# Channel shuffle on one core: twelve tiles of 38 KB in place of fifteen of 32, with two store buffers instead of three

## The chip, the cores and the metric

The kernel runs on one core of a Trainium2 chip; the other cores are idle. The metric is device time in microseconds (us), as the median of a few executions. The profile is of one execution; its span, from the first to the last instruction, is some 1.8 us shorter than the time.

"KB a partition" is how much of a tile lies in each of the 128 partitions: a tile of 32 KB is 128 rows of 32 KB, so 4096 KB in all.

## The reference

```python
x = x.reshape(batch, h, w, groups, channels_per_group)   # 16, 64, 64, 8, 32
x = x.transpose(0, 1, 2, 4, 3)
x = x.reshape(batch, h, w, c)                            # float32, c = 256
```

Nothing is computed. Each pixel's 256 channels are read as 8 groups of 32 and written as 32 groups of 8. 67.11 MB must come in and 67.11 MB must go out.

## The kernel before

A tile is loaded, VectorE copies it into another buffer in the new order, and it is stored. Loads are issued from SyncE, stores from ScalarE, so each has a queue of its own on the 16 DMA engines. The tile framework adds the waits: load n+3 waits for copy n (three load buffers), copy n waits for load n and for store n-3 (three store buffers).

```python
_SIZES = [4, 8, 16] + [32] * 15 + [4]     # KB a partition; sums to 512
_IN_BUFS = 3
_OUT_BUFS = 3
# ... (pools, views)
for q in _SIZES:
    in_tile = in_pool.tile([P, biggest * c], F32, name="in_tile")
    nc.sync.dma_start(out=in_tile[:, : q * c], in_=rows(x_flat, first, q))
    out_tile = out_pool.tile([P, biggest * c], F32, name="out_tile")
    nc.vector.tensor_copy(
        out=out_tile[:, : q * c].rearrange("p (i j g) -> p i j g", j=CPG, g=G),
        in_=in_tile[:, : q * c].rearrange("p (i g j) -> p i j g", g=G, j=CPG),
    )
    nc.scalar.dma_start(out=rows(out_flat, first, q), in_=out_tile[:, : q * c])
    first += P * q
```

## Time and profile before

| | before |
|---|---|
| time, median of 3 | 316.96 us |
| span of the profile | 315.2 us |
| VectorE busy | 119.9 us, 38% |
| packets of both queues, share of 16 engines' time | 49.8% + 49.4% |
| mean rate | 426 GB/s |
| DMAs | 19 loads, 19 stores |

The page's lines for these stand in the prediction. How to read them: look for the unit that is never free. VectorE isn't it; the DMA engines are, in all slices but the first and the last.

### The profile page before, as it was taken

To read this page: it belongs to the slowest core of one execution; us is meant where nothing else is said; L and a number is where in the kernel's file an instruction comes from. 1 tells how busy PE (TensorE), PEld (TensorE's weight loads), DVE (VectorE), ACT (ScalarE), POOL (GpSimd) and SP (SyncE) were. 2 spreads that over 40 slices of the span, in tenths; PEclk is the share of its full clock that TensorE was granted. 3 is DMA by queue.
4 is the path that set the end of the run, shared out by engine and by line. 5 is a ranking of instruction groups with operands and counts; after the bars stand their busy time and mean duration, and the time that the engine had idled before them with its cause. 6 is when DMAs were issued, how large, how long until landed. Compare 5 with 4: busy or idle time off the path is not lost.

```text
span 315.2 us, 150 instructions
## 1 busy us (share of the span) xinstructions
DVE 119.9 (38%) x19; POOL 0.2 (0%) x4
## 2 busy tenths in 40 slices
DVE  2419270905318062270722608135090440905500
POOL 0000000000000000000000000000000000000000
DMA  8999999999999999999999999999999999999996
GB/s 314 408 422 458 403 449 408 457 408 453 412 453 412 458 412 453 420 445 428 437 428 437 437 428 437 428 437 433 437 433 437 428 441 424 445 420 426 439 441 291
DMA packets 5472, 134.22 MB, mean 426 GB/s; under 512 B 608, under 2 KB 608, under 8 KB 1120
## 3 DMA queue, kind: packets, MB, share of 16 engines
q1 hardware_dynamic: 2736, 67.11, 49.8%
q10 hardware_dynamic: 2736, 67.11, 49.4%
HBM read 67.11 MB, written 67.11 MB: 426 GB/s over the span
## 4 chain that ended last, share of the span: by engine, by line
DMA 40%; another core or an unknown queue 30%; DVE 25%; issue 0%; DVEq 0%; SPq 0%
DMA in_tile<-in_x_dram 40%; DVE out_tile L49 25%; DVEq L49 0%; SPq L47 0%
## 5 line engine op out<-in xcount | busy, mean ns | idle before, releaser
L49 DVE COPY out_tile<-in_tile 128x8192 f32<-128x8192 f32 (+3 forms) x19 | 119.9, 6313 | 179.3 <-DMA in_tile<-in_x_dram 179.3
L71 POOL MEMSET const-uint8-127<- 128x1 uint8 x1 | 0.1, 103 | 0.0
L71 POOL MEMSET const-bfloat16-1.0<- 128x1 bf16 x1 | 0.1, 102 | 0.0
L71 POOL MEMSET const-float32-0.0<- 128x1 f32 x1 | 0.1, 99 | 0.2 <-issue 0.2
L71 POOL MEMSET const-float32-1.0<- 128x1 f32 x1 | 0.1, 99 | 0.0
## 6 DMA issues: line engine op xcount, KB each, us to landing
in_tile<-in_x_dram SPq DMA_DIRECT2D x15, 4096.0 KB, 50.5
out_dram<-out_tile ACTq DMA_DIRECT2D x15, 4096.0 KB, 42.4
in_tile<-in_x_dram SPq DMA_DIRECT2D x1, 2048.0 KB, 11.1
out_dram<-out_tile ACTq DMA_DIRECT2D x1, 2048.0 KB, 30.1
in_tile<-in_x_dram SPq DMA_DIRECT2D x2, 512.0 KB, 22.7
in_tile<-in_x_dram SPq DMA_DIRECT2D x1, 1024.0 KB, 5.5
out_dram<-out_tile ACTq DMA_DIRECT2D x2, 512.0 KB, 14.4
out_dram<-out_tile ACTq DMA_DIRECT2D x1, 1024.0 KB, 22.9
```

What stands on the lines that cost most here:

```text
L49: nc.vector.tensor_copy(out=out_tile[:, : q * c].rearrange("p (i j g) -> p i j g", j=CPG, g=G), in_=in_tile[:, : q * c].rearrange("p (i g ...
L71: nc = _bacc.Bacc("TRN2", target_bir_lowering=False, num_devices=1)
```

## The change

The intent: larger transfers, so fewer of them and less overhead, in the same memory. Three load and two store buffers of 38 KB take 190 KB a partition, where three and three of 32 KB took 192. The three small tiles ahead stay, the small one at the end goes.

```diff
-_SIZES = [4, 8, 16] + [32] * 15 + [4]
+_SIZES = [4, 8, 16] + [38] * 12 + [28]
 _IN_BUFS = 3
-_OUT_BUFS = 3
+_OUT_BUFS = 2
```

## The prediction

> **What bounds the kernel now.** I read the page first (busy shares, then the slices, then the queues), then the DMA view, the waits, the copies by shape, the timeline and at last windows over the end.
>
> From the page of the kernel before: busy time of the engines, the DMA share in 40 slices, and the two queues (q1 loads, q10 stores) with packets, MB and share of the 16 DMA engines' time.
>
> ```profile
> DVE 119.9 (38%) x19; POOL 0.2 (0%) x4
> ...
> DMA  8999999999999999999999999999999999999996
> ...
> q1 hardware_dynamic: 2736, 67.11, 49.8%
> q10 hardware_dynamic: 2736, 67.11, 49.4%
> ```
>
> VectorE, the only engine that computes, works 38% of the span. The DMA engines are at 90% or more in 38 of 40 slices, and the two queues' packets add up to 49.8 + 49.4 = 99.2% of all the time that 16 engines have in 315.2 us. So the kernel is bound by its transfers, and only the first and the last slice have room in them.
>
> The waits (us in total, times, longest) and the copies by shape (count, busy us, mean ns, idle before):
>
> ```profile
> DVE out_tile L49 <- DMA in_tile<-in_x_dram: 179.3, 19, 11.9
> ```
>
> ```profile
> L49 DVE COPY out_tile<-in_tile 128x8192 f32<-128x8192 f32 x15 | 111.9, 7459 | 166.2 <-DMA in_tile<-in_x_dram 166.2
> L49 DVE COPY out_tile<-in_tile 128x4096 f32<-128x4096 f32 x1 | 3.8, 3835 | 4.1 <-DMA in_tile<-in_x_dram 4.1
> ```
>
> All 19 waits of VectorE are put down to loads. None is put down to a store, so three store buffers are enough today. But a wait names only what came last; the DMA view (count, KB each, median us from issue to landing) shows how near the stores are:
>
> ```profile
> in_tile<-in_x_dram SPq DMA_DIRECT2D x15, 4096.0 KB, 50.5
> out_dram<-out_tile ACTq DMA_DIRECT2D x15, 4096.0 KB, 42.4
> ...
> out_dram<-out_tile ACTq DMA_DIRECT2D x2, 512.0 KB, 14.4
> ```
>
> A store is 42.4 us in flight, and in the timeline the copies start 19.4 us apart (267.84, 287.23). So a store buffer is held for 7.5 + 42.4 = 49.9 of the 58.1 us that three buffers allow. With two it could not be held so long: that is the risk of this change.
>
> The timeline of the last copies and two windows at the end (busy of VectorE, of GpSimd, clock, DMA share, GB/s):
>
> ```profile
> 267.84 7.45 DVE L49 COPY out_tile<-in_tile 128x8192 f32<-128x8192 f32 x1 [11.91 <-DMA in_tile<-in_x_dram]
> 287.23 7.47 DVE L49 COPY out_tile<-in_tile 128x8192 f32<-128x8192 f32 x1 [11.95 <-DMA in_tile<-in_x_dram]
> 298.20 1.09 DVE L49 COPY out_tile<-in_tile 128x1024 f32<-128x1024 f32 x1 [3.50 <-DMA in_tile<-in_x_dram]
> ```
>
> ```profile
> 300.00:305.00 5.00, 0.00 (x0) 0.00 (x0) 1.00 1.02 439
> 310.00:315.00 5.00, 0.00 (x0) 0.00 (x0) 1.00 0.55 229
> ```
>
> The last copy ends at 299.3 and the last packet of a store at 313.9 (packet records of the trace). For those 14.6 us the stores run alone, and they still move 439 GB/s: one queue fills the engines as well as two. So neither of the queues must be full; what costs time is only a stretch in which **both** are empty.
>
> **What the Trainium skill says.** Four places.
> 1. "DMA: Bandwidth & Descriptors", Where 436 GB/s comes from: it gives a ceiling of 435.2 GB/s for the 16 engines. The trace agrees: one tile in and one out, 2 x 4.194 MB every 19.36 us, is 433 GB/s. There is next to nothing above it.
> 2. The same page, Rules for kernel authors: for top bandwidth, 128 partitions and at least 1 MiB a DMA. The bulk transfers here are 4 MiB already, so the rule promises nothing for larger ones; the packet times below agree.
> 3. The same page, Queues, rings and completion order: an engine takes turns between its queues packet by packet. In the packet records one row of one partition is one packet, and the turns show: a 512 KB store takes 14.4 us (median) when its 4 KB rows alternate with much longer load rows. Eight rows an engine at 1.21 + 0.16 us a pair are 11.0 us, the rest is the way to the first packet and receipt.
> 4. "SBUF — State Buffer", Specifications (TRN2): 224 KiB a partition, about 208 usable. Before takes (3 + 3) x 32 = 192 KB, after (3 + 2) x 38 = 190 KB, so it fits. No run has yet shown it.
>
> **The change, part by part.**
>
> *Rows of 38 KB, fewer packets.* The packet records give fixed durations when the engines are full: 4 KB 159 ns, 8 KB 309, 16 KB 611, 32 KB 1213, and 9 ns for the completion packet of each engine and DMA. (1213 - 159) / 28 = 37.64 ns a KB, which leaves 159 - 4 x 37.64 = 8 ns fixed. A 38 KB row is then 8 + 38 x 37.64 = 1439 ns, a 28 KB row 1062 ns (estimates from that line). Each engine moves 8 rows of every DMA. Per queue and engine:
> before: 15 x 8 x 1.213 + 8 x (0.159 + 0.309 + 0.611 + 0.159) + 19 x 0.009 = 145.56 + 9.90 + 0.17 = 155.63 us;
> after: 12 x 8 x 1.439 + 8 x (0.159 + 0.309 + 0.611 + 1.062) + 16 x 0.009 = 138.14 + 17.13 + 0.14 = 155.41 us.
> Two queues: 311.27 against 310.82, so **0.45 us less**. All of this lies on the path, since the engines are full; but it is all that six DMAs fewer are worth.
>
> *Larger copies.* (7459 - 3835) / 4096 elements = 0.885 ns an element with 0.21 us fixed. A 38 KB tile (9728 elements) takes 8.82 us, a 28 KB tile (7168) 6.55 us. VectorE's sum falls from 119.9 by three fixed costs, about 0.6 us, to 119.3. The beat becomes 16 x 1.439 + 0.02 = 23.04 us, so the copy still fits in it. All beside the transfers: nothing.
>
> *Two store buffers.* Copy n now waits until store n-2 has landed. At the start the loads of 4, 8 and 16 KB land as before (by 12.4 us), but store 0, with 4 KB rows alternating with 38 KB load rows, lands at some 20 us, so the copy of the 16 KB tile starts near 20.5 instead of 12.74. Store 1 takes 8 x (1.439 + 0.309) = 14.0 us more, store 2 16.4 us, and from there on stores take 23.0 each. So the copies fall into step with the *stores*: store n-2 lands, copy n runs 8.8 us, store n queues behind store n-1. A store is then 2 x 23.04 - 8.8 - 0.5 = 37 us in flight. Meanwhile loads run ahead: at copy n two further loads are out or landed, and load n+3 is issued when the copy ends. While copy n runs, store n-1 has its packets in the queue. Both queues are never empty together, and what one leaves the other takes. Cost: 0 in the middle.
>
> *The end.* The last tile is 28 KB instead of 4. Loads finish first, then stores have the engines alone, and a 38 KB store takes 8 x 1.439 = 11.5 us. The chain that must fit beneath it: receipt of store n-2 to start of copy 0.5 us (as between last completion packet of a load and copy), copy 8.82, issue to first packet 1.1 us (the first load was issued at 0.73, its first packet is at 1.75). For tile 14 that is 10.4, for the last 6.55 + 1.6 = 8.2 us. Both are under 11.5, so the engines stay full: cost 0, with 1.1 us to spare at the tighter place.
>
> *Sum.* First packet at 1.75 as before; 310.82 us of packets; the 0.85 us of gaps that before has (first packet to last 312.12, less 311.27), which I take over; 1.28 us from the last packet to the end of the span: 314.7 against 315.2. The median has 1.8 us more than the span, so **316.5 us**.
>
> **Rivals.** (a) *The two store buffers starve the engines.* For it: 49.9 us of holding against 46.1 us that two buffers allow, so VectorE will certainly wait for stores. Against it: a wait of VectorE costs nothing while packets are queued, and by the reckoning above some always are. If the tighter place in the tail is missed by 2 us and the start loses 1 to 2, it comes to 318 to 320 us, still within 2%. (b) *The 28 KB tail is exposed*: if store 14 were done before the last copy is, up to the whole 8.2 us would show, 325 us, which is over 2% slower. It needs loads that finish last; the loads lead by nearly three tiles, so I hold it unlikely. (c) *Larger rows are faster, or slower, than the line says.* Faster by over 2% would need some 440 GB/s, more than any steady window has; 32 KB rows have only 8 of 1213 ns that could be saved. Slower (a long row cut into pieces, a row pitch that the memory likes less) nothing in the trace suggests.
>
> **Range and chances.** The sum gives 316.5; the runs of before spread by 0.3. Upward I leave room for a microsecond of gaps at start or end: 316.0 to 317.5. A gain of over 2% would need 310.6, below the packets' own time with the start and end: 1%. Over 2% slower needs rival (b) or a slow row: 2%.
>
> **What would show it.** Packets 16 x 144 = 2304 a queue; the share of the two queues again near 99%; copies at 8.8 us and 23.0 us apart. VectorE's waits should now be mostly on stores, while the DMA slices stay at 9; stores 37 us in flight, the copy of the 16 KB tile late at some 20 us. Wrong: a slice below 9 between the first and the last (then two buffers starve it), over half a microsecond of gap before the last store (then the tail is exposed), or 38 KB rows away from 1.44 us.

## The result, and the profile after

| | before | after |
|---|---|---|
| time, median of 4 (same rounds) | 316.82 us (316.46 to 317.02) | 316.75 us (316.41 to 317.20) |
| span of the profile | 315.2 us | 314.7 us |
| packets of a queue | 2736 | 2304 |
| VectorE busy | 119.9 us | 119.2 us |

The ratio of after to before is 1.0001, with a 95% interval of 0.9986 to 1.0016: the same.

The page after: DMA share in 40 slices, and the two queues (packets, MB, share of 16 engines).

```profile
DMA  8999999999999999999999999999999999999997
...
q1 hardware_dynamic: 2304, 67.11, 49.8%
q10 hardware_dynamic: 2304, 67.11, 49.4%
```

As before, no slice between the first and the last is below 9, and the shares of the queues are the same two numbers. The waits of VectorE after (us in total, times, longest us):

```profile
DVE out_tile L49 <- DMA out_dram<-out_tile: 175.9, 14, 14.6
DVE out_tile L49 <- DMA in_tile<-in_x_dram: 5.5, 2, 4.1
```

Before, all 19 waits were for loads, 179.3 us. Now 14 of 16 are for stores, and the total is 181.4. The wait has changed its name, hardly its length, and the time not at all. That is the main thing to see here: VectorE isn't the bound, it waits for whatever comes last, and here it didn't matter what that was.

The copies by shape and the DMA issues after (count, KB each, median us to landing):

```profile
L49 DVE COPY out_tile<-in_tile 128x9728 f32<-128x9728 f32 x12 | 105.6, 8802 | 158.2 <-DMA out_dram<-out_tile 158.2
L49 DVE COPY out_tile<-in_tile 128x7168 f32<-128x7168 f32 x1 | 6.5, 6545 | 5.9 <-DMA out_dram<-out_tile 5.9
```

```profile
in_tile<-in_x_dram SPq DMA_DIRECT2D x12, 4864.0 KB, 46.8
out_dram<-out_tile ACTq DMA_DIRECT2D x12, 4864.0 KB, 37.0
```

And parts of the timeline after (start, duration, idle before):

```profile
6.59 2.02 DVE L49 COPY out_tile<-in_tile 128x2048 f32<-128x2048 f32 x1 [1.42 <-DMA in_tile<-in_x_dram]
20.36 3.90 DVE L49 COPY out_tile<-in_tile 128x4096 f32<-128x4096 f32 x1 [11.75 <-DMA out_dram<-out_tile]
...
235.23 8.79 DVE L49 COPY out_tile<-in_tile 128x9728 f32<-128x9728 f32 x1 [14.13 <-DMA out_dram<-out_tile]
258.23 8.82 DVE L49 COPY out_tile<-in_tile 128x9728 f32<-128x9728 f32 x1 [14.21 <-DMA out_dram<-out_tile]
279.31 8.76 DVE L49 COPY out_tile<-in_tile 128x9728 f32<-128x9728 f32 x1 [12.26 <-DMA out_dram<-out_tile]
294.01 6.54 DVE L49 COPY out_tile<-in_tile 128x7168 f32<-128x7168 f32 x1 [5.95 <-DMA out_dram<-out_tile]
```

The copy of the 16 KB tile starts at 20.36 instead of 12.74, as it now waits for the 4 KB store; the later copies are 23.0 us apart; the last two waits get shorter, because the loads are through and the stores then have the engines alone.

### The profile page after: what moved, and what is told of

It is laid out like the page before. It is cut to its first block, busy times and chain, and to the rows that moved or that the text cites. A ratio compares the mean times of both kernels' runs of the same rounds, so it can differ in the third digit from the quotient of the medians.

```text
span 314.7 us, 133 instructions
## 1 busy us (share of the span) xinstructions
DVE 119.2 (38%) x16; POOL 0.2 (0%) x4
## 3 DMA queue, kind: packets, MB, share of 16 engines
q1 hardware_dynamic: 2304, 67.11, 49.8%
q10 hardware_dynamic: 2304, 67.11, 49.4%
## 4 chain that ended last, share of the span: by engine, by line
DMA 75%; DVE 20%; issue 0%; SPq 0%; DVEq 0%
DMA out_dram<-out_tile 74%; DVE out_tile L49 20%; DMA in_tile<-in_x_dram 2%; SPq L47 0%; DVEq L49 0%
## 5 line engine op out<-in xcount | busy, mean ns | idle before, releaser
L49 DVE COPY out_tile<-in_tile 128x9728 f32<-128x9728 f32 (+4 forms) x16 | 119.2, 7449 | 181.4 <-DMA out_dram<-out_tile 175.9
```

Of the source, the lines that this page charges most:

```text
L49: nc.vector.tensor_copy(out=out_tile[:, : q * c].rearrange("p (i j g) -> p i j g", j=CPG, g=G), in_=in_tile[:, : q * c].rearrange("p (i g ...
```

## The experiments

All kernels gave the correct result, and all edits are of the same three lines. In the packet records I also looked for **gaps**: stretches over 0.3 us in which no packet of any of the 16 engines was under way. Before and after have none. Note that a gap asks for all 16 engines at once: an engine that stands idle alone doesn't show in it. Windows list a row whole where it starts, so a share can exceed 1.00.

The theory: the time is the packets' time plus those gaps; who waits for whom is irrelevant as long as one of the two queues has packets. The rival: fewer store buffers cost, and the larger tiles pay that back, so that the two cancel out.

### Two store buffers alone

```diff
-_OUT_BUFS = 3
+_OUT_BUFS = 2
```

> The tile sizes of before (4, 8, 16, fifteen of 32 KB, 4), with two store buffers in place of three. My theory (a wait of VectorE costs nothing while packets are queued): as before within 0.3%, about 316.9 us, VectorE waiting for stores instead of loads, stores about 2 x 19.36 - 7.5 - 0.5 = 31 us in flight instead of 42. Rival (fewer store buffers starve the engines and the larger tiles pay that back): 318 to 325 us.

Measured: 316.74 us against 316.81, ratio 0.9999 (0.9986 to 1.0011). The waits and issues of this run:

```profile
DVE out_tile L49 <- DMA out_dram<-out_tile: 178.7, 17, 12.3
DVE out_tile L49 <- DMA in_tile<-in_x_dram: 5.6, 2, 4.1
```

```profile
out_dram<-out_tile ACTq DMA_DIRECT2D x15, 4096.0 KB, 31.1
```

The waits went over to the stores, stores are in flight for 31.1 us instead of 42.4, no gap, no cost. The rival falls: there is nothing that the larger tiles would have to pay back.

### One store buffer

```diff
 _SIZES = [4, 8, 16] + [38] * 12 + [28]
-_OUT_BUFS = 2
+_OUT_BUFS = 1
```

> The changed kernel with one store buffer instead of two. My theory: load n+3 and store n are both released by the end of copy n, take turns row by row and so end together, and with one store buffer copy n+1 begins only then: both queues are empty for 0.5 + 8.8 - (what of it overlaps) + 1.1, some 9 us of each beat, and over 10 us at the last tiles. Beat 32 us instead of 23, about 430 us (410 to 445). Rival (loads run ahead during the copy, so a single store buffer is hidden too, but for the end): 335 to 346 us. Rival (buffers never matter, bytes alone do): 317 us.

Measured: 481.14 us, ratio 1.5189 (1.5166 to 1.5213). The page's copies and DMA shares in 40 slices, then windows over one beat (share and GB/s are the last two columns):

```profile
DVE  0103070070070070070070070070070070062441
...
DMA  8994919919919919919919919919919909736447
```

```profile
135.00:140.00 5.00, 5.00 (x1) 0.00 (x0) 1.00 0.00 0
140.00:145.00 5.00, 3.71 (x1) 0.00 (x0) 1.00 0.44 93
145.00:150.00 5.00, 0.00 (x0) 0.00 (x0) 1.00 0.69 280
150.00:155.00 5.00, 0.00 (x0) 0.00 (x0) 1.00 1.04 451
```

Wherever VectorE is busy, the DMA engines rest. This is the wait that does cost. Copy n releases store n and load n+3 at the same moment; both are eight rows an engine, they take turns, and they land together (load and store both at 134.3 us, the next two both at 170.2). Then copy n+1 has the stage to itself. The records show 14 gaps, 137.9 us in all, and those of the steady beats are 10.4 us: the sum of the chain of receipt, copy and issue that the prediction worked out (0.5 + 8.8 + 1.1). The parts are a little different: from the last completion packet at 134.31 to the copy at 134.94 are 0.6 us, and from the end of the copy to the first packet at 144.70 are 1.0. The mechanism was right and the size was not: I had expected part of the chain to be covered, a beat of 32 us and some 430 us. The beat is 35.9 us. Of the 12.9 us above 23.0, 10.4 are the gap. Some 1.4 of the other 2.5 lie in the first pair of rows: the first load row of each engine after this gap lasts 2.1 to 3.4 us (2.8 in the mean), where 1.44 is usual. The window after it, at 280 GB/s, shows this in part; twelve of these rows started, and so count, in the window before. The rest I haven't broken down. At the end of this run, where stores alone start again after a gap, their first 38 KB rows last 1.45 to 1.46 us, so it is the loads that start slowly. Why they do I haven't tested.

### Another order of the tiles, with two and with three store buffers

```diff
-_SIZES = [4, 8, 16] + [32] * 15 + [4]
+_SIZES = [8, 16, 4] + [32] * 14 + [4, 32]
-_OUT_BUFS = 3
+_OUT_BUFS = 2        # the second run keeps 3
```

> The tiles of before in another order (8, 16, 4, fourteen of 32, then 4 and 32 KB last), with two store buffers. Same bytes, same packets, same number of DMAs. My theory: the copy of the last 32 KB tile waits for the store two tiles earlier, and only the 4 KB store (1.28 us) lies beside it: 0.5 + 7.46 + 1.1 - 1.28 = 7.8 us with both queues empty, about 324.7 us. Rival (bytes and DMA count alone): 317 us.

> The same order of tiles (4 and 32 KB last) with three store buffers. My theory: the last copy waits for a store one tile earlier and overlaps the 32 KB store before it: no gap, about 316.9 us, so 7.8 us less than with two buffers. Rival (the order of the tiles itself costs, for instance a large last store): the same 324 to 325 us as with two.

Measured: 326.56 us with two (ratio 1.0307, 1.0293 to 1.0321) and 317.61 with three (1.0025, 1.0011 to 1.0038). The end of the two timelines, two buffers first:

```profile
295.47 1.09 DVE L49 COPY out_tile<-in_tile 128x1024 f32<-128x1024 f32 x1 [13.51 <-DMA out_dram<-out_tile]
305.05 7.50 DVE L49 COPY out_tile<-in_tile 128x8192 f32<-128x8192 f32 x1 [8.48 <-DMA out_dram<-out_tile]
```

```profile
276.63 1.09 DVE L49 COPY out_tile<-in_tile 128x1024 f32<-128x1024 f32 x1 [3.37 <-DMA in_tile<-in_x_dram]
296.05 7.47 DVE L49 COPY out_tile<-in_tile 128x8192 f32<-128x8192 f32 x1 [18.32 <-DMA in_tile<-in_x_dram]
```

With two buffers the last copy starts nine microseconds later, because it waits for the store of the 32 KB tile two before it, and only a 4 KB store lies beside it. The records show one gap of 7.62 us, from 305.79 on, where 7.8 were expected. And in the windows of the two-buffer run that gap is plain:

```profile
300.00:305.00 5.00, 0.00 (x0) 0.00 (x0) 1.00 0.84 359
305.00:310.00 5.00, 4.95 (x1) 0.00 (x0) 1.00 0.04 15
```

With three buffers there is no gap. So the same bytes, packets and number of DMAs differ by 8.95 us, of which 7.6 are the gap; 1.0 more was lost on the way there (the last packet of the 4 KB store is at 305.8 instead of 304.8). The three-buffer run is also 0.7 us above what I had expected, and the two-buffer run 1.9; what lies outside the gap is not explained. So two store buffers *can* cost, but only through what is left to cover the last copies.

### The changed kernel with its last two tiles swapped

```diff
-_SIZES = [4, 8, 16] + [38] * 12 + [28]
+_SIZES = [4, 8, 16] + [38] * 11 + [28, 38]
```

> The changed kernel with its last two tiles swapped (28, then 38 KB). My theory: the chain under the last store but one is 0.5 + 8.8 + 1.1 = 10.4 us and the 28 KB store beside it lasts 8 x 1.062 = 8.5, so a gap of 1.9 us: about 318.5 us, a size of exposure between none (the changed kernel) and 7.8 us (4 KB before 32). Rival (order within the large tiles is free): 316.7 us.

Measured: 318.55 us, ratio 1.0064 (1.0047 to 1.0081): small, but clear of noise. One gap, 1.66 us from 302.06 on, where the sum said 1.9. So the cover under the last copy is a matter of plain arithmetic: an 11.5 us store beside an 8.2 us chain leaves nothing (the changed kernel), 8.5 beside 10.4 leaves 1.7, 1.3 beside 9.1 leaves 7.6.

### The price of a row by itself

```diff
-_SIZES = [4, 8, 16] + [32] * 15 + [4]
-_IN_BUFS = 3
-_OUT_BUFS = 3
+_SIZES = [4] * 128
+_IN_BUFS = 24
+_OUT_BUFS = 24
```

> All tiles 4 KB (128 of them, 24 load and 24 store buffers, so that no buffer holds anything up): the packet cost alone. By the line of 8 ns and 37.64 ns a KB, with 9 ns per completion packet: 2 x (128 x 8 x 0.159 + 128 x 0.009) = 327.9 us of packets an engine, against 311.3: about 333.6 us, 5% slower. Rival (larger rows are worth more than the line says, so the change gained on packets and lost on buffers): clearly over 336 us.

Measured: 327.97 us, ratio 1.0359 (1.0344 to 1.0375). Rows eight times as short cost 11.35 us, where my line gave 16.7. The page shows why the line was too steep: the shares of the two queues add up to over 100%.

```profile
q1 hardware_dynamic: 18432, 67.12, 50.6%
q10 hardware_dynamic: 18432, 67.12, 50.2%
```

An engine's records of short rows overlap a little, so their durations (159 ns) are more than what each adds. Worked backwards: 1744 more rows an engine (2048 less 304) cost 11.35 us, at most 6.5 ns each, the completion packets included. The change has 48 rows an engine fewer (304 less 256), so at that price it is worth 0.31 us, not 0.45. This is an estimate: the price is a mean from 4 to 32 KB, and nothing shows that rows of 32 and 38 KB overlap as those of 4 KB do. Either is too small to be seen in times that spread by 0.6 to 0.8.

### Equal tiles, and what the small tiles at the start are for

By the theory the small tiles at either end should be worth nothing.

```diff
-_SIZES = [4, 8, 16] + [32] * 15 + [4]
+_SIZES = [32] * 16
```

> Sixteen equal tiles of 32 KB, three and three buffers, no small tiles at either end. My theory: as loads keep the engines busy from the first packet and the last copy hides beneath the store before it (0.5 + 7.46 + 1.1 = 9.1 against 9.7 us), the small tiles are worth nothing and the time is 316.4 to 316.9 us. Rival (the small tiles at the ends are what keeps start and end short): a start or an end exposed by up to 9 us, 320 to 326 us.

Measured: 324.24 us, ratio 1.0245 (1.0217 to 1.0273). The theory missed, and the rival in the form that it had: there is no gap. Two things are different. The first is the rate all along: in a window from 40 to 280 us, this run and then before:

```profile
40.00:280.00 240.00, 90.03 (x12) 0.00 (x0) 1.00 1.00 425
```

```profile
40.00:280.00 240.00, 94.81 (x13) 0.00 (x0) 1.00 1.00 433
```

The share says 1.00 in both, so the engines have packets open, yet in this one they are slower. Load rows last 1.26 us in the mean instead of 1.22, and the 16 engines drift apart: the completions of one load lie within 0.7 us at the start and 7.2 us apart at the end, where before has 1.1 to the end. A DMA has landed when its last engine is done, so the slowest sets the beat, 20.0 us instead of 19.4.

The second is the end. DMA share in 40 slices of the equal tiles:

```profile
DMA  8999999999999999999999999999999999999866
```

Before has a single slice below 9 there. The quickest engine has its part of the last load at 295.1 us, the slowest at 302.3, and only then the last copy starts; so the engines that are ahead run out of work, one by one, which isn't a gap by my count. The records added up show both: 317.0 us of packets an engine against 312.6 before, but 321.1 from first packet to last against 312.1. So of the 9.0 us between these two profiles about half is in longer rows and about half in engines that stand idle.

Three theories were told apart (here and below, edits are shown against the sixteen equal tiles unless the changed kernel's sizes stand in them):

```diff
-_SIZES = [32] * 16
+_SIZES = [4, 8, 16, 4] + [32] * 15     # small at the start alone
```

> Why sixteen equal tiles cost 324.2 us and not 316.7 is open: its packets are slower (mean load row 1.26 us instead of 1.21) and the engines drift apart. Here: small tiles at the start alone (4, 8, 16, 4 KB, then fifteen of 32), three and three buffers. All large tiles start at multiples of 4 MiB, as with the equal tiles. Theory A (without small tiles at the start the rows of loads and stores run in a bad step): fast, 316.5 to 317.5 us. Theory B (the address of the large tiles, multiples of 4 MiB on both sides): slow, 322 to 326 us. Theory C (it is the small tile at the end that is missed): slow, 322 to 326 us.

```diff
-_SIZES = [32] * 16
+_SIZES = [32] * 15 + [28, 4]           # small at the end alone
```

> Fifteen tiles of 32 KB, then 28 and 4: small at the end alone, three and three buffers. Theory A (start): slow, 322 to 326 us. Theory B (addresses): slow, 322 to 326 us. Theory C (end): fast, 316.5 to 317.5 us.

```diff
-_SIZES = [4, 8, 16] + [38] * 12 + [28]
+_SIZES = [38] * 13 + [18]              # the changed kernel without the small start
```

> The changed kernel's large tiles without the small ones ahead: thirteen of 38 KB and one of 18, three load and two store buffers. Theory A (start): slow, 320 to 328 us. Theory B (addresses at multiples of 4 MiB): fast, 316.3 to 317.5 us, as 38 KB tiles start at multiples of 4.75 MiB. Theory C (end): fast, as the last tile is the smaller one.

Measured: the small start alone 316.90 us (ratio 1.0005, 0.9988 to 1.0021), the small end alone 324.69 us (1.0246, 1.0226 to 1.0265). That leaves the start and rules out the end and the addresses. The 38 KB tiles without a small start took 346.44, 346.87 and 347.02 us in three runs and 318.96 in one: it has two behaviours of its own (three are over 1.5% above the fourth, so there is no ratio). Both are slower than the changed kernel's slowest run, 317.20, at a clock of 1.000 throughout. The page of one of its slow runs:

```profile
DMA  8999999999999999999999999989999997771982
```

The completions of one load lie 0.9 us apart for the first, 20.2 us for the sixth and 39 us for the eleventh: up to the sixth, the quickest engine keeps the 23.0 us beat and the slowest needs some 28. Here idle engines are the larger part: 321.0 us of packets an engine in the 341.6 from first to last. So the start probably matters for the change as well, and the change kept it; as the same kernel also ran once at 318.96, and only slow runs show the large loss, that is not shown.

How much of a start is needed, and does a small tile help later?

```diff
-_SIZES = [32] * 16
+_SIZES = [4, 28] + [32] * 15
```

> How much of a small start is needed: one tile of 4 KB, one of 28, then fifteen of 32, three and three buffers. The start theory says that the first store must fall beside load rows of another length, so that the turns of the two queues are out of step from the beginning: a single small tile does that, 316.5 to 317.5 us. Rival (it takes the loads a lead of several tiles, as three small tiles give): slow, 320 to 326 us.

```diff
-_SIZES = [32] * 16
+_SIZES = [32, 32, 32, 4, 28] + [32] * 12
```

> The same sizes as the run above, but 4 and 28 KB come fourth and fifth, after three of 32. Start theory in its narrow form (a bad step is broken by any small tile): the beats are 20.0 us up to the small tile and 19.4 after it, the engines stop drifting apart, 317 to 319 us. Rival (what the first store does decides for good): 323 to 326 us with 20.0 us beats to the end.

Measured: 316.99 us (ratio 1.0003, 0.9985 to 1.0021) with one small tile ahead, so one is enough, and the rival of a long lead falls. Moved three tiles back, the same tile gives 322.11 us (1.0174, 1.0133 to 1.0215; slower, though not clearly by 2%): better than none, but its beats after the small tile are still 19.7 us and the drift goes on, to 3.4 us at the last load. So neither of the two expectations holds in full: a later small tile doesn't break the bad step, and the first store doesn't decide everything either. In the run with one small tile ahead, load and store land within 0.1 us of each other on every beat and nothing is slow, so "in step" is not the cause by itself. In the slow kernels at 23 to 27 us, where the first long store rows begin, load rows are up to 0.9 us longer on nearly all engines. But that is not what sets them apart: with one small tile ahead, load rows at 23.3 to 23.7 us are up to 0.65 us longer on all 16 engines too. In that run and in before no 32 KB load row that starts after 70 us lasts over 1.26 us; in the run of equal tiles 211 do, on to the end. **Why they go on, and why the engines drift apart, stays open**.

No run beat before and after by more than noise, and with these bytes I see little left to gain: from first packet to last they are 312.1 and 311.8 us without a gap.

## Why the prediction was right

Point by point, as the prediction put them:

- **The bound and the packet line.** 38 KB rows were to last 1439 ns and 28 KB rows 1062; the records' medians are 1439 and 1062. The first packet of the run is at 1.73 and the last ends at 313.5; the span is 314.7 as summed, the median 316.75 against 316.5.
- **"0.45 us less".** The term with the weakest ground. Short packets' records overlap slightly, and at the price of the run with 4 KB rows the saving would be 0.31 us (an estimate). The profile's span fell by 0.5, which the spread of 0.6 to 0.8 between runs doesn't allow me to call a gain.
- **The 0.85 us "of gaps".** The sum took them over from before, and they came through, but they are no gaps: the records have none. Many load rows of the first stretch are longer than the line (the 16 KB ones last 672 ns in the mean, not 611), and the engines don't start and end together. The number held because the change left the start as it was.
- **Larger copies.** 8.82 and 6.55 us were worked out, 8.80 and 6.545 measured, the sum 119.2 for 119.3. All of it lies beside the transfers.
- **Two store buffers, cost 0.** The sequence came as described: the 16 KB copy at 20.36 (expected 20.5), beats of 23.0, stores 37.0 us in flight, waits on stores. The run with two store buffers alone shows that this costs nothing; the one with a single buffer shows what it looks like when both queues do run dry, at 10.4 us a beat.
- **The end, cost 0 with 1.1 us to spare.** The changed kernel has no gap. Taking the cover away in two sizes brought gaps of 1.66 and 7.62 us, within 0.3 of the sums. There is some luck in the parts: 0.73 to 1.75 us is 1.0 of issue, not the 1.1 of the prediction, and receipt took 0.4 us in the changed kernel and 0.6 with one store buffer, not 0.5. The slips are small beside the 1.1 us to spare.
- **The rivals.** (a), starving, was rightly weighed: VectorE does wait, at no cost. (b), the exposed tail, needs another order of tiles, as the swapped run shows. (c) was weighed on too little: "nothing in the trace suggests" slow rows holds for the changed kernel, but without the small tiles ahead a kernel of 32 KB rows was 7.6 us slower and one of 38 KB rows some 30 in three of four executions, in part by longer rows and in part by engines that stood idle. The prediction used the steady row times of before as if they belonged to the row length alone, and took the 16 engines as one; both also depend on how the queues start. In this it was lucky: the change left that start as it was.

## What to carry to other kernels

In a kernel bound by transfers, add up the packets' time and look for stretches with both queues empty, and compare the completions of one load over the engines, since engines that drift apart stand idle without such a stretch. In these runs a new wait of the compute engine cost nothing until it made such a stretch. To size buffers, compare the chain receipt + copy + issue with the transfer that lies beside it, above all at the end, where little is left to cover it. Before removing small leading tiles that seem useless, measure: here one of 4 KB (and one of 28, to keep the sum) is worth 7 us.

## What the Trainium skill lacked or had wrong

- "DMA: Bandwidth & Descriptors", Rules for kernel authors, recommends at least 1 MiB a DMA for top bandwidth. It doesn't say what less costs when many are under way: with 24 buffers each way, 512 KB DMAs with 4 KB rows lost 3.6% (327.97 us against 316.62). And 4 MiB DMAs were no guarantee: sixteen equal ones lost 2.4% (324.24 us).
- The same page, Where 436 GB/s comes from, says that about 358 GB/s of memory bandwidth binds for transfers between HBM and SBUF. With one core running that doesn't hold here: loads and stores together held 433 GB/s over 240 us. (The same paragraph has a measured 425 GB/s, which agrees better.)
- No page that I read tells of the drift: without a small tile ahead, the 16 engines came apart by 7.2 us (32 KB rows) and, in the profiled slow run, by up to 39 us (38 KB rows), and the time rose by 7.6 and, in three executions of four, by some 30 us. One tile of 4 KB ahead, and one of 28, removed it with 32 KB rows. The cause is open.
- No page that I read has a figure for loads that start from empty queues: with one store buffer, the first load row of each engine after a gap lasted 2.1 to 3.4 us (at 144.7 us), where 1.44 is usual.
